# The rest of the modulation of a diffusion block: its weight chunks in buffers of their own

## The chip, the cores and the metric

One core of one Trainium2 chip. Times are device microseconds (us) of one execution, median of the runs shown. The engines are named as in the profile: PE (TensorE, with PEld for its weight loads), DVE (VectorE), ACT (ScalarE), POOL (GpSimd) and SP (SyncE, which here only issues DMA transfers).

## The reference

One layer of a diffusion model on 256 latent tokens with 256 context tokens, width 2048, in fp32. A conditioning vector gives six modulation rows; they enter at three places of the layer:

```python
silu_c = jax.nn.silu(c)
mod_l = jnp.split((silu_c @ w_mod[l] + b_mod[l])[:, None, :], 6, axis=-1)
...
y_ctx, y_lat = token_mixer(modulate(ctx, mod_c[0], mod_c[1]), modulate(x, mod_l[0], mod_l[1]),
                           rows, need_ctx, w_in[l], hy_p, ml_p, s5_p, out_p)
x = layer_norm(DEEPNORM_ALPHA * x + mod_l[2] * y_lat, ln1_g[l], ln1_b[l])
x = layer_norm(DEEPNORM_ALPHA * x + mod_l[5] * sq_relu_mlp(modulate(x, mod_l[3], mod_l[4]), w_ff1[l], w_ff2[l]),
               ln2_g[l], ln2_b[l])
```

`w_mod` is 2048 x 12288. The mixer projects its input with `w_in`, runs three branches (Hyena: long convolution; mLSTM; S5: a state-space scan), and merges them: `merged = g_hy * (y_hy @ w_hy_out) + g_ml * (y_ml @ w_ml_out) + g_s5 * (y_s5 @ w_s5_out)`, then `merged @ w_out`. The MLP is `square(relu(h @ w1)) @ w2` with 8192 hidden units. The first two modulation rows are needed at once; `mod_l[2]` after `w_out`, `mod_l[3]` and `mod_l[4]` after the first layer norm, `mod_l[5]` after the MLP's first `w_ff2` block.

## The kernel before, in words

All weights come from DRAM in chunks of 128 partitions x 1024 columns, 512 KB each, and are used once. A chunk of a matmul's weights is loaded by SP (`raw`, L200) into a tile `wr`, of which the pool `wp` has four buffers. ACT rounds it to the matmul's type (`wh`, L190), DVE subtracts to keep the rest (`wl`, L194), and PE does three products for each pair of operands, 24 matmuls of 256 columns for one chunk (L211). A `wr` buffer comes free when ACT and DVE have read it.

The rest of the modulation, rows 2 to 5 (8192 columns, 16 blocks of 512 columns, 8 chunks to a block, 128 chunks), does not go to PE as weights: it is a product with one vector. DVE does it, two instructions for a chunk, each 128 x 512: `acc = w * c` (L1178) for the first, `acc = w * c + acc` (L1180) for the others, called "macs" below. The sum over partitions is one matmul with ones into `px`, and the block's result goes to `mrow` in DRAM or to `mcol` (L1189, L1197). The chunk's load is the same `raw`, so it takes one of the four `wr` buffers. There is one accumulator tile, `mac`.

`mod_late` is a generator; `chunk_done` advances it after each weight chunk of the matmuls, by a rate that the stages set (0.3 to 1.75 chunks for each weight chunk). In what order the instructions then stand on each engine is decided by a scheduler, which simulates the program while it is built; each engine works in its order, SP's transfers too.

The stages that matter here, in order of time: pool pB holds the Hyena columns of `w_in`, the injection of inputs into the scan (`s5_inject`, last copy to the scan's inputs at L641), the scan itself (63 steps of four POOL instructions, L651 to L654; its first reader on DVE is L679, on PE L686), gate columns, and the scan's output with a gated linear unit. Pool pC holds the Hyena convolutions, the rest of the gate columns and three merges (products at L1231 and L1233). The tail, with pool ffp, does `w_out` (`residual`, L1276 and L1277, reads x in a `wr` tile, L1270), the first norm (aggregate L1288), ff1 and ff2 (`relu2`, with the square at L1354). The code asks for modulation blocks where they are used: `need_mods(12)` at the head of the tail, `drain(1)` between ff1 and ff2.

Of the kernel before, what the change touches and what calls it, by code (L numbers as in the profile page):

```python
# [17 lines left out]
P = 128  # L18
# [97 lines left out]
class Kern:  # L116
    def __init__(self, ctx, tc, I, out, dbg=None):
        self.tc, self.nc, self.I, self.out, self.dbg = tc, tc.nc, I, out, dbg or {}
        pool = lambda name, bufs, **k: ctx.enter_context(tc.tile_pool(name=name, bufs=bufs, **k))
        self.ctx = ctx  # L120
        self.cst = pool("cst", 1)
        self.wp = pool("wp", 3)
        self.t32p = pool("t32p", 2)
        self.sm = pool("sm", 2)
        self.ps = pool("ps", 2, space=bass.MemoryType.PSUM)
        self.dr = pool("dr", 1, space=bass.MemoryType.DRAM)
        self.n = 0
        self.sides = [[None, 0.0, 0.0] for _ in range(3)]
        self.bank, self.both = "aux", False
        self.mods = 0  # L130


    def nm(self, s):
# [1029 lines left out]
    def mod_late(self):  # L1163


        nc = self.nc
        v = nc.vector
        w = self.I["w_mod"][0]
        for b in range(16):
            c0 = 2 * D + b * 512  # L1170
            acc = self.t(self.sm, [P, 512], "mac", 1)
            for k0 in range(0, KT, 2):
                wt = self.raw(w, k0, 2, c0, 512)
                for kk in range(2):
                    k = k0 + kk
                    x, c = wt[:, kk], self.sc[:, k:k + 1]
                    if k == 0:
                        v.tensor_scalar(acc, x, c, None, op0=ALU.mult)  # L1178
                    else:
                        v.scalar_tensor_tensor(acc, x, c, acc, op0=ALU.mult, op1=ALU.add)  # L1180
                if k0 + 2 < KT:
                    yield
            which = b // 4
            if which in (0, 3):
                ps = self.aux([1, 512], "px")
                self.mm(ps, self.ones, acc, True, True)
                brow = self.b2([1, 512])
                nc.gpsimd.dma_start(brow, self.I["b_mod"][0:1, c0:c0 + 512])
                v.tensor_add(brow, brow, ps)  # L1189
                o = (b % 4) * 512  # L1190
                nc.gpsimd.dma_start(self.mrow[which // 3:which // 3 + 1, o:o + 512], brow)
            else:
                ps = self.aux([P, 4], "px")
                for j in range(4):
                    self.mm(ps[:, j:j + 1], acc[:, j * P:(j + 1) * P], self.ones, j == 0, True)
                o = (b - 4) * 4
                v.tensor_add(self.mcol[:, o:o + 4], ps, self.bmod[:, 32 + b * 4:36 + b * 4])  # L1197
            self.mods = b + 1
            yield

    def need_mods(self, n):
        while self.mods < n:
            next(self.sides[1][0])
# [42 lines left out]
    def tail(self, merged):  # L1246
        nc, I = self.nc, self.I
        v = nc.vector
        self.ffp = self.ctx.enter_context(self.tc.tile_pool(name="ffp", bufs=1))
        self.need_mods(12)  # L1250
        m2 = self.row(self.mrow[0:1, :], "rowa")
        x1 = self.t(self.ffp, [P, 2, D], "x1")
# [153 lines left out]
    def run(self):  # L1406
# [56 lines left out]
        with self.scope("yp") as self.yp:  # L1463
# [49 lines left out]
                self.mlstm_out()  # L1513
            steps = self.lin_w_steps(w_in, O_MG, 3 * D, KT, lat, self.mg_consume)
            with self.scope("pB") as self.br:
                self.n6 = 5
                hy = self.lin_w_steps(w_in, O_HY, 3 * W, KT, lat, self.hy_consume)
                self.run_steps(hy, 6)
                self.s5_inject()
                self.sides[1][1] = 0.3  # L1520
                self.with_side(self.s5_scan(), 2)
                self.run_steps(hy, 36)
                self.run_steps(steps, 32)
                self.with_side(self.s5_output(), 0.6)
                self.run_steps(steps, 48)
                self.drain()
                self.s5_glu()
            with self.scope("pC") as self.br:
                self.n6 = 7
                self.hyena()  # L1530
                self.run_steps(steps, 96)
                self.merge(1, I["w_ml_out"][0], self.y_ml, first=True)
                self.merge(2, I["w_s5_out"][0], self.y_s5)
                self.merge(0, I["w_hy_out"][0], self.y_hy, last=True)
        self.tail((self.mh, self.ml))

    def run_steps(self, steps, n):
# [35 lines left out]
```

## Time and profile before

| | us |
|---|---|
| median of 3 runs | 2005.19 (2005.02 to 2005.46) |
| profiled execution | 2014.18 |
| its span | 2012.4 |
| PE busy | 1870.4 (93%) |
| DVE busy | 1300.5 (65%) |
| ACT busy | 803.2 (40%) |
| POOL busy | 361.7 (18%) |

Busy shares are means over the span; the span has stages with different limits. A wait is the idle time of an engine ahead of an instruction, put down to what came last. 455.92 MB were moved, 227 GB/s over the span.

### The profile page before, as it was taken

The numbers are of one execution on the slowest core, as the hardware profiler recorded it, in microseconds if no ns is written. First come the engines' busy times: TensorE is split into PE (matmuls) and PEld (weight loads), VectorE is DVE, ScalarE is ACT, GpSimd is POOL, SyncE is SP. The second block draws the span as 40 slices with busy tenths as digits, with TensorE's granted clock in tenths as the row PEclk, the third lists the DMA queues.
The fourth block names the chain that finished last, engine by engine and source line by source line (L and its number), as shares of the span: only waits on it lengthen the run. The fifth ranks groups of instructions, "written<-read, shape, count | busy, mean of one in ns | idle before, by whom it ended". The sixth has DMA issues, their size and how long they took to land.

```text
span 2012.4 us, 34496 instructions
## 1 busy us (share of the span) xinstructions
PE 1870.4 (93%) x13945; PEld 1707.4 (85%) x13945; DVE 1300.5 (65%) x1810; ACT 803.2 (40%) x1063; POOL 361.7 (18%) x534
## 2 busy tenths in 40 slices
PE   5888999999997995999889998999999999999996
PEld 1666988989997995999779877999988899998985
DVE  8985777647866553556786866766755555555556
ACT  2433324226543333544234533444433344444332
POOL 1221101000019994000452400400000000000001
PEclk7898999999998997999999998999999999999998
DMA  9997667775797765677657866577765566666553
GB/s 346 339 344 262 192 202 220 227 208 174 232 349 230 239 222 210 226 254 259 244 180 253 276 225 227 158 240 224 254 224 187 187 183 186 181 186 231 190 188 105
DMA packets 253472, 455.92 MB, mean 227 GB/s; under 512 B 28597, under 2 KB 75349, under 8 KB 251776
## 3 DMA queue, kind: packets, MB, share of 16 engines
q1 hardware_dynamic: 221824, 382.43, 59.4%
q0 software_dynamic: 14112, 50.83, 7.0%
q10 hardware_dynamic: 17376, 20.45, 3.1%
q8 instruction: 109, 1.79, 0.4%
q14 instruction: 51, 0.42, 0.1%
HBM read 424.75 MB, written 32.05 MB: 227 GB/s over the span
## 4 chain that ended last, share of the span: by engine, by line
PE 67%; DMA 10%; DVE 9%; POOL 8%; issue 3%; ACT 2%; SPq 0%; ACTq 0%; POOLq 0%; DVEq 0%
PE mm L211 59%; PE aux L211 4%; DMA wr<-in_w_mod_dram 4%; DVE wl L194 3%; DMA wr<-in_w_in_dram 2%; POOL sc L651 2%; POOL sc L653 2%; POOL sc L652 2%; POOL t L654 2%; DMA wr<-in_w_out_dram 1%; ACT wh L190 1%; PE px L406 1%; PE px L211 1%; PE aux L214 1%; DVE mac L1180 1%
## 5 line engine op out<-in xcount | busy, mean ns | idle before, releaser
L211 PE MATMUL mm<-t,wh 128*128 128x256 f32 x5888 | 1101.7, 288 | 29.0 <-ACT wh L190 18.1
L211 PEld LDWEIGHTS mm<-t,wh 128*128 128x128 f32 x5888 | 932.2, 194 | 49.6 <-ACT wh L190 19.9
L194 DVE TENSOR_TENSOR wl<-wr,wh 128x1024 fp32r<-128x1024 f32 (+1 forms) x517 | 649.6, 1263 | 385.9 <-ACT wh L190 385.4
L190 ACT ACTIVATE wh<-wr 128x1024 fp32r<-128x1024 f32 (+1 forms) x517 | 545.9, 1058 | 811.0 <-PE mm L211 580.6
L211 PE MATMUL mm<-t,wl 128*128 128x256 f32 x2944 | 847.6, 288 | 13.9 <-DVE wl L194 13.8
L211 PEld LDWEIGHTS mm<-t,wl 128*128 128x128 f32 x2944 | 570.1, 194 | 25.9 <-DVE wl L194 18.3
L1180 DVE SCALAR_TENSOR_TENSOR mac<-wr,vecs,mac 128x512 f32<-128x512 f32 x240 | 185.3, 772 | 156.5 <-DMA wr<-in_w_mod_dram 153.8
L211 PE MATMUL mm<-wh,t 128*128 128x512 f32 (+1 forms) x960 | 249.1, 349 | 0.2
L211 PEld LDWEIGHTS mm<-wh,t 128*128 128x128 f32 x960 | 169.0, 190 | 24.2 <-ACT wh L190 1.6
L211 PE MATMUL mm<-wl,t 128*128 128x512 f32 (+1 forms) x480 | 168.0, 350 | 5.5 <-DVE wl L194 5.5
L211 PE MATMUL mm<-wh,ff 128*128 128x512 f32 (+1 forms) x576 | 155.3, 358 | 0.0
L211 PEld LDWEIGHTS mm<-wh,ff 128*128 128x128 f32 x576 | 101.7, 188 | 17.6
L211 PEld LDWEIGHTS mm<-wl,t 128*128 128x128 f32 x480 | 91.3, 190 | 20.5 <-DVE wl L194 9.2
L211 PE MATMUL mm<-wl,ff 128*128 128x512 f32 (+1 forms) x288 | 103.0, 357 | 0.0
L211 PE MATMUL mm<-ty,wh 128*128 128x256 f32 x384 | 73.3, 289 | 0.0
L1402 POOL DMA_DIRECT2D t<-in_ln_g_dram x1 | 0.5, 535 | 355.0 <-PE mm L211 355.0
L211 PE MATMUL mm<-ty,wl 128*128 128x256 f32 x192 | 56.4, 294 | 7.6 <-DVE wl L194 7.5
L211 PEld LDWEIGHTS mm<-wl,ff 128*128 128x128 f32 x288 | 54.2, 188 | 8.8
L211 PEld LDWEIGHTS mm<-ty,wh 128*128 128x128 f32 x384 | 60.7, 192 | 0.9
L406 PE MATMUL px<-wr,b 128*32 128x512 f32 x128 | 41.4, 739 | 18.1 <-DVE s5t L335 10.5
L211 PE MATMUL aux<-t,t 128*128 128x384 f32 (+3 forms) x160 | 47.3, 411 | 7.7 <-DVE t L1146 3.2
L211 PEld LDWEIGHTS mm<-ty,wl 128*128 128x128 f32 x192 | 36.9, 192 | 9.1 <-DVE wl L194 8.4
(384 smaller groups left out, 1621.6 us busy)
## 6 DMA issues: line engine op xcount, KB each, us to landing
wr<-in_w_ff_dram SPq DMA_DIRECT2D x256, 512.0 KB, 3.9
wr<-in_w_in_dram SPq DMA_DIRECT2D x192, 512.0 KB, 4.7
wr<-in_w_mod_dram SPq DMA_DIRECT2D x160, 512.0 KB, 4.8
wr<-in_w_out_dram SPq DMA_DIRECT2D x32, 512.0 KB, 4.7
wh<-in_w_mod_dram SPq DMA_DIRECT2D x16, 512.0 KB, 7.6
wl<-in_w_mod_dram SPq DMA_DIRECT2D x16, 512.0 KB, 7.1
QD<-s5Q POOLq DMA_DIRECT2D x12, 512.0 KB, 7.1
WA<-s5wa POOLq DMA_DIRECT2D x24, 256.0 KB, 6.2
```

The costliest lines, as they stand in the source:

```text
L190: return self.nc.scalar.activation(out, in_, f, bias=bias, scale=scale)
L194: self.nc.vector.tensor_sub(lo, x, hi.bitcast(F32))
L211: self.nc.tensor.matmul(out, lhsT, rhs, start=start, stop=stop, skip_group_check=True)
L214: self.nc.tensor.transpose(out, in_, self.c("ident", n)[:, :n])
L406: nc.tensor.matmul(ps[o:o + 32], self.st[:, k, :], raw[:, kk, :], start=k < 4, stop=k >= KT - 4, skip_group_check=True, tile_position=(0, o))
L651: v.tensor_mul(t1, self.a8[:, 0], S[:, :, :, :, n - 1])
L652: v.tensor_mul(t2, self.a8[:, 1], S[:, :, ::-1, :, n - 1])
L653: v.tensor_add(t1, t1, S[:, :, :, :, n])
L654: v.tensor_add(S[:, :, :, :, n], t1, t2)
L1180: v.scalar_tensor_tensor(acc, x, c, acc, op0=ALU.mult, op1=ALU.add)
L1402: nc.gpsimd.dma_start(g2r, I["ln2_g"].to_broadcast([P, D]))
```

## The change

Modulation chunks get a tile of their own, `wm`, from the pool of the stage: two buffers in pB, one in pC, two in the tail. Outside these stages (`modp` is None) they use `wr` as before. The four `wr` buffers then hold only the matmuls' weights (and x). In pB one line that set the number of `t6` buffers goes; no `t6` tile is taken there. 77 of the 128 modulation loads use `wm`: 38 in pB, 16 in pC, 23 in the tail. The lines of the new file from L131 on are one higher, from `mod_raw` on ten; the load of `wm` is L1208.

```diff
--- before.py
+++ after.py
@@ -128,6 +128,7 @@
         self.sides = [[None, 0.0, 0.0] for _ in range(3)]
         self.bank, self.both = "aux", False
         self.mods = 0
+        self.modp = None
 
 
     def nm(self, s):
@@ -1170,7 +1171,7 @@
             c0 = 2 * D + b * 512
             acc = self.t(self.sm, [P, 512], "mac", 1)
             for k0 in range(0, KT, 2):
-                wt = self.raw(w, k0, 2, c0, 512)
+                wt = self.mod_raw(w, k0, c0)
                 for kk in range(2):
                     k = k0 + kk
                     x, c = wt[:, kk], self.sc[:, k:k + 1]
@@ -1198,6 +1199,15 @@
             self.mods = b + 1
             yield
 
+    def mod_raw(self, w, k0, c0):
+
+        if self.modp is None:
+            return self.raw(w, k0, 2, c0, 512)
+        pool, bufs = self.modp
+        raw = self.t(pool, [P, 1024], "wm", bufs).rearrange("p (k c) -> p k c", k=2)
+        self.nc.sync.dma_start(raw, w[k0 * P:(k0 + 2) * P, c0:c0 + 512].rearrange("(k p) c -> p k c", p=P))
+        return raw
+
     def need_mods(self, n):
         while self.mods < n:
             next(self.sides[1][0])
@@ -1247,6 +1257,7 @@
         nc, I = self.nc, self.I
         v = nc.vector
         self.ffp = self.ctx.enter_context(self.tc.tile_pool(name="ffp", bufs=1))
+        self.modp = (self.ffp, 2)
         self.need_mods(12)
         m2 = self.row(self.mrow[0:1, :], "rowa")
         x1 = self.t(self.ffp, [P, 2, D], "x1")
@@ -1513,7 +1524,7 @@
                 self.mlstm_out()
             steps = self.lin_w_steps(w_in, O_MG, 3 * D, KT, lat, self.mg_consume)
             with self.scope("pB") as self.br:
-                self.n6 = 5
+                self.modp = (self.br, 2)
                 hy = self.lin_w_steps(w_in, O_HY, 3 * W, KT, lat, self.hy_consume)
                 self.run_steps(hy, 6)
                 self.s5_inject()
@@ -1525,13 +1536,16 @@
                 self.run_steps(steps, 48)
                 self.drain()
                 self.s5_glu()
+                self.modp = None
             with self.scope("pC") as self.br:
                 self.n6 = 7
+                self.modp = (self.br, 1)
                 self.hyena()
                 self.run_steps(steps, 96)
                 self.merge(1, I["w_ml_out"][0], self.y_ml, first=True)
                 self.merge(2, I["w_s5_out"][0], self.y_s5)
                 self.merge(0, I["w_hy_out"][0], self.y_hy, last=True)
+                self.modp = None
         self.tail((self.mh, self.ml))
 
     def run_steps(self, steps, n):
```

The scheduler makes other orders of it. Ahead of the scan's first reader (L679, after L680) on DVE, before the change (`mac` is the accumulator, the number a block or tile):

```order
L194 TENSOR_TENSOR wl_8242<-wr_8239,wh_8241 128x1024
L1197 TENSOR_TENSOR mcol_79<-px_8145,vecs_93 128x4
L1178 TENSOR_SCALAR mac_8352<-wr_8353,vecs_93 128x512
L194 TENSOR_TENSOR wl_8272<-wr_8269,wh_8271 128x1024
L1180 SCALAR_TENSOR_TENSOR mac_8352<-wr_8353,vecs_93,mac_8352 128x512
L194 TENSOR_TENSOR wl_8360<-wr_8357,wh_8359 128x1024
L1180 SCALAR_TENSOR_TENSOR mac_8352<-wr_8553,vecs_93,mac_8352 128x512
L194 TENSOR_TENSOR wl_8390<-wr_8387,wh_8389 128x1024
L1180 SCALAR_TENSOR_TENSOR mac_8352<-wr_8553,vecs_93,mac_8352 128x512
L194 TENSOR_TENSOR wl_8473<-wr_8470,wh_8472 128x1024
L679 TENSOR_TENSOR b_1109_8182<-t_677_5292,sign_85 64x4x32 x4
```

The same place after the change:

```order
L195 TENSOR_TENSOR wl_8360<-wr_8357,wh_8359 128x1024
L1181 SCALAR_TENSOR_TENSOR mac_8352<-wm_8790,vecs_93,mac_8352 128x512
L195 TENSOR_TENSOR wl_8390<-wr_8387,wh_8389 128x1024
L1181 SCALAR_TENSOR_TENSOR mac_8352<-wm_8790,vecs_93,mac_8352 128x512
L1181 SCALAR_TENSOR_TENSOR mac_8352<-wm_8885,vecs_93,mac_8352 128x512
L195 TENSOR_TENSOR wl_8473<-wr_8470,wh_8472 128x1024
L1181 SCALAR_TENSOR_TENSOR mac_8352<-wm_8885,vecs_93,mac_8352 128x512
L195 TENSOR_TENSOR wl_8560<-wr_8557,wh_8559 128x1024
L1181 SCALAR_TENSOR_TENSOR mac_8352<-wm_8986,vecs_93,mac_8352 128x512 x2
L195 TENSOR_TENSOR wl_8597<-wr_8594,wh_8596 128x1024
L1181 SCALAR_TENSOR_TENSOR mac_8352<-wm_9110,vecs_93,mac_8352 128x512 x2
L680 TENSOR_TENSOR b_1109_8182<-t_677_5292,sign_85 64x4x32 x4
```

Over the same number of rows, macs of two chunks stood among the subtractions ahead of the reader, and of four now; two more subtractions stand there than before (`wl_8560`, `wl_8597`).

At the head of the `w_out` stage, DVE before the change (`mac_11442` is the last block that `need_mods(12)` asks for, `mac_12364` the first of the last four, `t_1571` the merged operand):

```order
L194 TENSOR_TENSOR wl_12247<-wr_12244,wh_12246 128x1024
L194 TENSOR_TENSOR wl_12275<-wr_12272,wh_12274 128x1024
L194 TENSOR_TENSOR t_1571_11762<-t_1344_10182,t_1571_11762 128x1024
L1189 TENSOR_TENSOR b_1642_12268<-b_1642_12268,px_12266 1x512
L194 TENSOR_TENSOR wl_12293<-wr_12290,wh_12292 128x1024
L194 TENSOR_TENSOR wl_12311<-wr_12308,wh_12310 128x1024
L194 TENSOR_TENSOR wl_12331<-wr_12328,wh_12330 128x1024
L1178 TENSOR_SCALAR mac_12364<-wr_12365,vecs_93 128x512
L1180 SCALAR_TENSOR_TENSOR mac_12364<-wr_12365,vecs_93,mac_12364 128x512
L194 TENSOR_TENSOR wl_12349<-wr_12346,wh_12348 128x1024
L194 TENSOR_TENSOR wl_12383<-wr_12380,wh_12382 128x1024
L194 TENSOR_TENSOR wl_12401<-wr_12398,wh_12400 128x1024
```

After the change, from the same subtraction on:

```order
L195 TENSOR_TENSOR wl_12247<-wr_12244,wh_12246 128x1024
L195 TENSOR_TENSOR wl_12275<-wr_12272,wh_12274 128x1024
L1181 SCALAR_TENSOR_TENSOR mac_11442<-wm_12262,vecs_93,mac_11442 128x512
L195 TENSOR_TENSOR t_1571_11762<-t_1344_10182,t_1571_11762 128x1024
L1181 SCALAR_TENSOR_TENSOR mac_11442<-wm_12262,vecs_93,mac_11442 128x512
L195 TENSOR_TENSOR wl_12293<-wr_12290,wh_12292 128x1024
L195 TENSOR_TENSOR wl_12311<-wr_12308,wh_12310 128x1024
L1190 TENSOR_TENSOR b_1642_12268<-b_1642_12268,px_12266 1x512
L1179 TENSOR_SCALAR mac_12364<-wm_12365,vecs_93 128x512
L195 TENSOR_TENSOR wl_12331<-wr_12328,wh_12330 128x1024
L1181 SCALAR_TENSOR_TENSOR mac_12364<-wm_12365,vecs_93,mac_12364 128x512
L1181 SCALAR_TENSOR_TENSOR mac_12364<-wm_12470,vecs_93,mac_12364 128x512
```

The last two macs of `mac_11442`, which stood ahead of this place before, now stand behind two subtractions of `w_out`'s chunks, and the next block's first mac stands behind four subtractions of `w_out` instead of five.

SP's queue at the same place, before:

```order
L1270 DMA wr_12326<-in_x_dram 128x2x512
L200 DMA wr_12328<-in_w_out_dram 128x2x512
L200 DMA wr_12346<-in_w_out_dram 128x2x512
L200 DMA wr_12365<-in_w_mod_dram 128x2x512
L200 DMA wr_12380<-in_w_out_dram 128x2x512
L200 DMA wr_12398<-in_w_out_dram 128x2x512
L200 DMA wr_12416<-in_w_out_dram 128x2x512
L200 DMA wr_12434<-in_w_out_dram 128x2x512
L200 DMA wr_12452<-in_w_out_dram 128x2x512
L200 DMA wr_12470<-in_w_mod_dram 128x2x512
L200 DMA wr_12474<-in_w_out_dram 128x2x512
L1270 DMA wr_12492<-in_x_dram 128x2x512
```

After:

```order
L1208 DMA wm_12262<-in_w_mod_dram 128x2x512
L1208 DMA wm_12365<-in_w_mod_dram 128x2x512
L1281 DMA wr_12326<-in_x_dram 128x2x512
L201 DMA wr_12328<-in_w_out_dram 128x2x512
L1208 DMA wm_12470<-in_w_mod_dram 128x2x512
L201 DMA wr_12346<-in_w_out_dram 128x2x512
L201 DMA wr_12380<-in_w_out_dram 128x2x512
L201 DMA wr_12398<-in_w_out_dram 128x2x512
L1208 DMA wm_12577<-in_w_mod_dram 128x2x512
L201 DMA wr_12416<-in_w_out_dram 128x2x512
L1208 DMA wm_12673<-in_w_mod_dram 128x2x512
L201 DMA wr_12434<-in_w_out_dram 128x2x512
```

Where two modulation loads stood among twelve transfers, five do now; the first two follow each other. Counted over the whole order on DVE: between the last merge product and the norm's first aggregate there are 8 macs before and 43 after; between the aggregate and ff1's first square 2 before and 7 after; behind that square 38 before and none after. Between the last state-input copy (L641) and the first reader of the scan there are 28 before and 41 after; while the inputs are injected 6 and 13. On PE, 46 weight chunks stand between the injection's last matmul and the scan's first reader before, 49 after. The number of instructions on each engine stays the same.

## Rows read from the trace of the kernel before

**Rows 1.** page, part 4: shares of the chain that ended last

```profile
PE 67%; DMA 10%; DVE 9%; POOL 8%; issue 3%; ACT 2%; SPq 0%; ACTq 0%; POOLq 0%; DVEq 0%
```

**Rows 2.** busy time by stage; columns PE, PEld, DVE, ACT, POOL, PEclk, DMA share, GB/s

```profile
545.00:600.00 55.00, 53.82 (x724) 52.57 (x724) 35.89 (x86) 28.29 (x57) 5.40 (x8) 1.00 1.00 344
600.00:780.00 180.00, 143.65 (x1148) 141.06 (x1148) 95.35 (x97) 59.85 (x74) 164.95 (x270) 0.91 0.64 211
...
930.00:1150.00 220.00, 196.96 (x1469) 184.99 (x1468) 167.75 (x200) 89.14 (x116) 83.38 (x85) 0.97 0.72 239
1150.00:1248.00 98.00, 88.63 (x462) 73.94 (x460) 63.28 (x79) 35.97 (x35) 3.89 (x4) 0.97 0.69 223
1248.00:1290.00 42.00, 35.20 (x254) 32.97 (x255) 37.98 (x57) 22.52 (x40) 26.07 (x20) 0.87 0.51 162
```

**Rows 3.** PE's waits, 600 to 780 us: total, times, longest

```profile
PE aux L686 <- POOL sc L651: 21.4, 1, 21.4
```

**Rows 4.** POOL's instructions, 601 to 778 us: busy us, mean ns | idle before

```profile
L652 POOL TENSOR_TENSOR sc<-t 128x96 f32<-128x96 f32 x63 | 44.0, 698 | 0.0
L653 POOL TENSOR_TENSOR sc<-sc,t 128x96 f32<-128x96 f32 x63 | 42.7, 678 | 0.1
L651 POOL TENSOR_TENSOR sc<-t 128x96 f32<-128x96 f32 x63 | 42.0, 666 | 7.8 <-DVE t L641 3.2
L654 POOL TENSOR_TENSOR t<-sc,sc 128x96 f32<-128x96 f32 x63 | 31.0, 493 | 4.5
```

**Rows 5.** timeline, 632 to 635.3 us: start, duration

```profile
631.75 0.40 PE L211 MATMUL mm<-t,wh 128*128 128x256 f32 x2
...
632.11 0.40 PE L211 MATMUL mm<-t,wh 128*128 128x256 f32 x2
...
632.12 2.79 DVE L194 TENSOR_TENSOR wl<-wr,wh 128x1024 fp32r<-128x1024 f32 x2
...
633.79 1.43 POOL L652 TENSOR_TENSOR sc<-t 128x96 f32<-128x96 f32 x1
```

**Rows 6.** timeline of POOL, 770 to 774 us, no DVE work beside it

```profile
773.05 0.44 POOL L652 TENSOR_TENSOR sc<-t 128x96 f32<-128x96 f32 x1
```

**Rows 7.** DVE's waits, 930 to 1150 us

```profile
DVE mac L1180 <- DMA wr<-in_w_mod_dram: 29.9, 11, 5.0
```

**Rows 8.** PE's waits, 930 to 1150 us

```profile
PE mm L211 <- DVE wl L194: 15.3, 9, 4.1
```

**Rows 9.** DVE's instructions, 1150 to 1248 us: busy us, mean ns | idle before

```profile
L194 DVE TENSOR_TENSOR wl<-wr,wh 128x1024 fp32r<-128x1024 f32 x33 | 42.0, 1276 | 24.6 <-ACT wh L190 24.5
...
L1180 DVE SCALAR_TENSOR_TENSOR mac<-wr,vecs,mac 128x512 f32<-128x512 f32 x7 | 5.3, 751 | 7.2 <-DMA wr<-in_w_mod_dram 7.1
```

**Rows 10.** DMA issues, 1150 to 1248 us: count, KB each, median us to landing

```profile
wr<-in_w_mod_dram SPq DMA_DIRECT2D x4, 512.0 KB, 5.2
```

**Rows 11.** DMA issues, 550 to 600 us

```profile
wr<-in_w_mod_dram SPq DMA_DIRECT2D x4, 512.0 KB, 7.5
```

**Rows 12.** timeline of DVE: four squares of the MLP, L1354

```profile
1289.69 1.22 DVE L1354 TENSOR_TENSOR b<-b 128x1024 f32<-128x1024 f32 x1
...
1453.96 1.21 DVE L1354 TENSOR_TENSOR b<-b 128x1024 f32<-128x1024 f32 x1
...
1655.70 1.22 DVE L1354 TENSOR_TENSOR b<-b 128x1024 f32<-128x1024 f32 x1
...
1816.98 1.22 DVE L1354 TENSOR_TENSOR b<-b 128x1024 f32<-128x1024 f32 x1
```

**Rows 13.** timeline of DVE at both ends of the w_out stage

```profile
1146.73 1.22 DVE L194 TENSOR_TENSOR wl<-wr,wh 128x1024 fp32r<-128x1024 f32 x1
1147.87 0.74 DVE L1180 SCALAR_TENSOR_TENSOR mac<-wr,vecs,mac 128x512 f32<-128x512 f32 x1
1148.53 1.28 DVE L1233 TENSOR_TENSOR mg<-mm,mg 128x512 f32<-128x512 f32 x2
...
1248.20 0.58 DVE L1288 BATCH_NORM_AGGREGATE l1mv<-lnst 128x2 f32<-128x48 f32 x2
```

## The prediction

> **What bounds the kernel now.** I read the chain of waits first: TensorE (PE) makes 67% of the chain that ended last, DMA 10%, VectorE (DVE) 9% and GpSimd (POOL) 8% [rows 1]. So the kernel is a matmul stream whose gaps are made by late weight chunks, by DVE, and once by the state-space scan on POOL. Then I read the busy time by stage, since the average over the span hides where each limit stands [rows 2]. The reader is to see three kinds of stage there. In 545 to 600 us the DMA share is 1.00 at 344 GB/s: nothing more can be fetched. In 600 to 780 POOL is busy 164.95 of 180 us with the scan, and PE waits 21.4 us at one place for its last step [rows 3]. In 930 to 1150 (hyena, gate columns, merges) and 1150 to 1248 (`w_out`) PE has 23 us and 9.4 us of gaps, and no engine is full. In ff1 (1289.69 to 1453.96) 7 blocks take 164.3 us, against 161.3 us for the same 7 blocks from 1655.70 to 1816.98 [rows 12], so the modulation work that lies in ff1 costs at most 3 us there.
>
> The two ops a chunk of the rest of the modulation ("macs", 0.75 us each) wait for their load: in 930 to 1150 DVE stands 29.9 us in 11 waits for one [rows 7], in 1150 to 1248 another 7.1 us [rows 9].
>
> **What the change does.** No instruction is added or taken away. 77 of the 128 modulation loads (38 in pB, 16 in pC, 23 in the tail) leave the rotation of four `wr` buffers for one of their own, two buffers deep (one in pC). The scheduler then places loads and macs earlier. Counted from the orders: 38 macs stand behind the first relu2 of ff1 before and none now; between the last merge product and the norm's first aggregate there are 8 before and 43 now. So the question is what the macs cost in the stages into which they move.
>
> *Scan.* Between the last state-input copy and the scan's first reader on DVE stand 28 macs before and 41 now, and 2 more `wl` subtractions. Beside DVE's subtraction of 1.40 us a scan step takes 1.43 us [rows 5], alone 0.44 [rows 6]: 0.99 us lost, 0.71 of DVE's time. The whole scan says the same: 159.7 us for 252 steps [rows 4], where 252 of 0.44 are 110.9 us, so 49 us are lost to DVE. 13 macs × 0.75 and 2 × 1.40 us are 12.5 us of DVE work, times 0.71 is 8.9 us by which the scan ends later. But PE's order has 3 more weight chunks ahead of the scan's first reader (49 for 46). Matmuls start three to 0.36 us [rows 5], so 24 of a chunk take 2.88 us, three 8.6 us: PE has that much more to do inside the 21.4 us for which it now waits. I take **0**; from below −6 (the scan is not slowed by macs that fall into gaps of its own) to +4 (macs block it for their whole length).
>
> The row shows a step that loses 0.71 of the DVE instruction beside it. The Trainium skill, page "SBUF — State Buffer", section "Who interferes with whom", says that a DVE instruction with two SBUF inputs contends with a GpSimd instruction that reads SBUF, and that the loser of that lock blocks for the other's whole instruction. By it the added DVE work would cost 12.5 us in place of 8.9, and this term would be +3.9 in place of 0; the trace lies under the rule.
>
> *Injection into the scan's state.* 7 more macs (13 for 6), so 3.5 more loads of 512 KB (1.8 MB) are asked of a stretch at 344 GB/s [rows 2], in which a load lands 7.5 us after its issue [rows 11]: 1.8 MB are 5.3 us of a full DMA. The loads are only earlier, the weight chunks' turn comes later, and part is made up in 600 to 780, where the share is 0.64. I take **+1** (0 to +5).
>
> *Hyena and merges.* The macs there are about as many as before. With one buffer a load cannot start before the second mac of the chunk ahead is done, so the wait for landing stays; the 29.9 us of DVE waits [rows 7] should not shrink much. What improves is the weight side: four `wr` buffers hold weights alone. PE loses 15.3 us to late `wl` [rows 8]. I take about half of that, **−7**; the bounds are −20 (both kinds of waits shrink) and +5 (a load that waits for its single buffer holds the weight loads behind it on SP).
>
> *`w_out`.* This is the largest term. DVE is busy 63.28 of 98 us [rows 2], with 24.5 us of waits for `wh` and 7.1 for loads [rows 9]: 95 of 98. 35 more macs at 0.72 us (between the 0.75 of one and the 0.67 from start to start) are 25 us, so DVE is busy 88 of 98 before any wait. Now the waits. Two buffers mean that a load is issued at the earliest when the second mac two chunks earlier is done, and it lands 5.2 us later [rows 10]. In the new order of DVE, in ten of the twenty such gaps of the stage, two subtractions and two macs stand between; started back to back these take 2 × 1.14 + 2 × 0.67 = 3.6 us (starts of ops that touch: 1146.73 to 1147.87 and 1147.87 to 1148.53 [rows 13]), so DVE stands about 1.6 us each time, 15 us in all; the first load of the stage is issued behind four loads of `w_out` and adds about 5. So 88 + 20 = 108 us for 98: **+10**. The bounds: 0, if the subtractions' old waits and these are the same gaps seen from the other side, as far as PE's 88.63 us of busy time permits; +22, if landing rises from 5.2 to 7.5 us, because 18 more loads are 9.4 MB in 98 us, which takes 223 GB/s to about 319, near the 344 at which the DMA was full [rows 2].
>
> *Norm.* PE is short of work here, 35.20 of 42 us [rows 2], and waits for DVE and ACT. Between the aggregate and ff1's first square stand 7 macs for 2; 5 of 0.75 us are **+4** (+1 to +8, beside POOL's 26 us of multiplies, where an op on DVE may be stretched as the subtraction of 1.40 us was).
>
> *ff1.* The 38 macs are gone: **−3** [rows 12]. Nothing more is to be had, as PE never stops.
>
> Sum: 0 + 1 − 7 + 10 + 4 − 3 = **+5 us**. The profiled execution took 2014.18 us with a span of 2012.4, and the median of the runs is 2005.19, so 9 us lie between profile and timing. The terms are a few waits each and do not grow with that, so I put the sum on the median: **2010 us** (and about 2019 in a profiled execution).
>
> **The rivals.** *Faster:* loads in buffers of their own run ahead of their macs. What speaks for it: the waits of 29.9 and 7.1 us are just those that a deeper prefetch removes, and in `w_out` DVE has 35 us of gaps to hold 25 us of macs. The chain holds waits for modulation loads only as a part of DMA's 10%. Price: half of PE's gaps in 930 to 1248 go (32/2 = 16) with −3 in ff1 and the scan's reader unchanged, +4 left in the norm: −15, 1990 us; all gaps gone, about −30. It decides where the DVE waits in `w_out` stay under the 10 us that DVE has left (98 − 88). Against it: two buffers are 3.6 us of lead for 5.2 us of landing.
> *Same:* gains in pC and ff1 meet the loss in `w_out`, or PE, 88.63 of 98 us, hides half of it: −7 + 1 + 5 + 4 − 3, within 4 us of 2005.
> *Slower by more:* DMA fills in `w_out`. At a landing of 7.5 us the ten short gaps are 2.3 us longer each, 23 us; half of it may fall together with weight chunks that are as late, so this term is +22 in place of +10. With +4 more in the injection: about 2026 us.
> *The scan blocked for whole instructions:* the scan ends 12.5 us later, while PE has 8.6 us more to do; +4 on the sum, 2014 us. The 1.43 us step beside a subtraction of 1.40 speaks against it. This is the rule of the Trainium skill's page "SBUF — State Buffer" cited above.
> *The change does nothing:* the loads would have to be held back by something other than buffers. The orders differ at 77 loads, so no more than a few hundredths.
>
> **How the numbers follow.** 0.2% (4 us) is about what a measurement can tell from no change. My forecast (+5, from +4 to +14) gets 0.32, the DMA-full case 0.12, the blocked scan 0.05: slower 0.49. Same 0.17, with the change that does nothing inside. Faster 0.34, since the waits that the change aims at are real, and a model in which DVE's old and new waits add up may count one gap twice. The range reaches from 1987, past the faster case's middle of 1990, to 2031, past the DMA-full case; the likeliest case's own is 2009 to 2019.
>
> **What would show it.** Right: 1150 to 1248 grows to about 108 us between the last merge product (1148.53) and the first aggregate (1248.20) [rows 13], with DVE over 80% busy, waits of mac for `wm` of 15 to 25 us, and DMA near 320 GB/s; seven blocks of ff1 at 161 us; the wait for the scan's last step smaller by about as much as the weight chunks took; PE's wait for `wl` in the hyena and merges under 10 us. Wrong: `w_out` at 98 us or less with few waits for `wm` (then two buffers were enough, and the faster case holds), a landing of 7 us there (then the DMA is full), or a scan that ends over 10 us later with PE idle. What would make the whole prediction wrong is above all that the macs fit into DVE's gaps in `w_out`, as then the largest term is gone and the sum falls to −5.

## The result, and the profile after

The changed kernel takes 2023.34 us (median of 5 runs, 2022.75 to 2026.8) where the kernel before takes 2005.02 (2003.93 to 2005.46): ratio 1.0096, 95% interval 1.0082 to 1.0111. It is 18 us slower. The direction was forecast and the time lies in the stated range (1987 to 2031), but the forecast was 2010: the sum of +5 us is less than a third of what came, and 2023 lies outside the 2009 to 2019 that the likeliest case was given.

The first profiled execution of the kernel before (2014.18 us) lay 9 us above its median, so I profiled it once more (e1 below: 2008.01 us, span 2006.2). From here on "before" in a comparison of stages is that second profile, where the first is not named. The span after is 2021.6, 15.4 us more, and the stages, cut at the same instructions in both, give it to the tail:

| stage, from instruction to instruction | before (e1) | after | difference |
|---|---|---|---|
| start to last copy of the scan's inputs | 599.2 | 601.0 | +1.8 |
| to the last product of the gated linear unit | 341.7 | 342.1 | +0.4 |
| to the last merge product | 204.4 | 202.0 | −2.4 |
| `w_out`: to the first aggregate | 96.1 | 106.8 | +10.7 |
| norm: to ff1's first square | 41.2 | 51.7 | +10.5 |
| ff1: to its 8th square | 165.7 | 159.9 | −5.8 |
| the rest | 557.9 | 558.1 | +0.2 |

The chain that ended last, page of the changed kernel (against [rows 1]: DMA's share falls from 10 to 6%, PE's rises):

```profile
PE 71%; DVE 9%; POOL 9%; DMA 6%; issue 3%; ACT 2%; POOLq 0%; DVEq 0%; ACTq 0%; SPq 0%
```

Busy time by stage of the changed kernel, to be set beside [rows 2]; columns as there:

```profile
545.00:600.00 55.00, 55.00 (x736) 53.80 (x735) 37.18 (x87) 25.30 (x50) 3.43 (x5) 1.00 1.04 370
600.00:785.00 185.00, 147.72 (x1180) 144.41 (x1181) 111.44 (x117) 63.11 (x79) 174.01 (x274) 0.92 0.70 230
...
930.00:1146.00 216.00, 194.47 (x1445) 183.64 (x1444) 169.82 (x196) 87.11 (x114) 86.66 (x85) 0.96 0.72 238
1146.00:1252.00 106.00, 93.30 (x476) 76.39 (x474) 85.82 (x115) 36.36 (x35) 2.34 (x4) 0.96 0.91 301
1252.00:1304.00 52.00, 39.33 (x268) 37.40 (x269) 44.27 (x63) 22.71 (x40) 27.90 (x22) 0.82 0.44 146
1304.00:1464.00 160.00, 160.00 (x1317) 158.51 (x1316) 85.08 (x72) 71.30 (x69) 1.03 (x2) 1.00 0.64 192
```

The reader is to see `w_out` (fourth line here): DVE busy 85.82 of 106 us where it was 63.28 of 98, and DMA at 301 GB/s where it was 223. The norm (fifth) holds 10 us more, PE is idle for a larger part of it, and the mean granted clock of the stretch is 0.82 where it was 0.87.

The same stages of e1, the second profile of the kernel before:

```profile
1145.30:1241.40 96.10, 88.58 (x466) 73.24 (x464) 63.62 (x81) 36.46 (x35) 4.59 (x4) 1.00 0.70 232
1241.40:1282.60 41.20, 34.58 (x252) 32.28 (x253) 38.55 (x57) 22.34 (x40) 26.33 (x20) 0.88 0.49 160
1282.60:1448.30 165.70, 164.22 (x1335) 160.43 (x1335) 109.82 (x112) 72.05 (x70) 1.01 (x2) 1.00 0.74 238
```

The waits of DVE in `w_out` after the change, and what it did there (against [rows 9]):

```profile
DVE mac L1181 <- DMA wm<-in_w_mod_dram: 12.4, 9, 3.3
DVE wl L195 <- ACT wh L191: 7.1, 9, 1.7
```

```profile
L195 DVE TENSOR_TENSOR wl<-wr,wh 128x1024 fp32r<-128x1024 f32 x33 | 41.2, 1255 | 7.1 <-ACT wh L191 7.1
L1181 DVE SCALAR_TENSOR_TENSOR mac<-wm,vecs,mac 128x512 f32<-128x512 f32 x40 | 29.9, 748 | 12.8 <-DMA wm<-in_w_mod_dram 12.4
```

24.5 us of waits for `wh` have become 7.1, 5.3 us of macs 29.9. A `wm` load lands in 5.0 us, as a modulation load did before [rows 10]:

```profile
wm<-in_w_mod_dram SPq DMA_DIRECT2D x21, 512.0 KB, 5.0
```

At the end of `w_out` one of these waits stands in the way. PE's last product, DVE's next instructions:

```profile
1243.71 0.28 PE L212 MATMUL mm<-wh,t 128*128 128x256 f32 x1
```

```profile
1246.77 0.75 DVE L1181 SCALAR_TENSOR_TENSOR mac<-wm,vecs,mac 128x512 f32<-128x512 f32 x1 [3.29 <-DMA wm<-in_w_mod_dram]
1247.43 0.75 DVE L1287 TENSOR_TENSOR b<-mm,rowa 128x256 f32<-128x256 f32 x2
```

The product is done at 1243.99, but DVE reads it (`residual`, L1287) only at 1247.43, behind a mac that waited 3.29 us for its load.

In the norm the macs stand between the pieces that PE's transposes and products wait for, while POOL multiplies. DVE's timeline there, then POOL's:

```profile
1257.58 0.74 DVE L1181 SCALAR_TENSOR_TENSOR mac<-wm,vecs,mac 128x512 f32<-128x512 f32 x1
...
1260.19 1.78 DVE L1181 SCALAR_TENSOR_TENSOR mac<-wm,vecs,mac 128x512 f32<-128x512 f32 x1
1261.89 1.85 DVE L195 TENSOR_TENSOR t<-b,t 128x256 fp32r<-128x256 f32 x2
1263.66 1.77 DVE L1181 SCALAR_TENSOR_TENSOR mac<-wm,vecs,mac 128x512 f32<-128x512 f32 x1
```

```profile
1258.71 2.71 POOL L1351 TENSOR_TENSOR x<-x,rowa 128x512 f32<-128x512 f32 x2 [3.02 <-PE aux L215]
1262.01 2.87 POOL L1352 TENSOR_TENSOR x<-x,rowb 128x512 f32<-128x512 f32 x2 [0.59 <-DMA rowb<-in_ln_b_dram]
```

A mac that starts before POOL's multiplies takes 0.74 us; those that start 0.24 or 0.25 us after one of them take 1.77 or 1.78. PE then waits for DVE's pieces, 9.2 us in all after its first transposes against 3.5 in e1, and behind such waits its granted clock falls. Two of the waits, and the clock (the third column from the right) after the first of them:

```profile
1275.71 0.58 PE L212 MATMUL mm<-t,wh 128*128 128x256 f32 x1 [2.12 <-DVE t L195]
1287.58 0.39 PE L212 MATMUL mm<-t,wh 128*128 128x256 f32 x1 [2.53 <-DVE t L195]
```

```profile
1275.70:1280.70 5.00, 4.99 (x23) 4.99 (x24) 2.22 (x4) 0.72 (x2) 0.00 (x0) 0.50 0.71 204
```

The clock is at 0.50, the level of 1.2 GHz, from 1274.4 to 1281.2 and again from 1288.1 to 1291.5 us. In e1 it stays at 1.00, 2.4 GHz, from 1251.4 us to the end of the norm:

```profile
1251.40:1282.60 31.20, 28.06 (x227) 26.97 (x226) 29.60 (x28) 16.43 (x28) 22.81 (x17) 1.00 0.38 110
```

### The profile page after: what moved, and what is told of

It reads as the page before. It is cut to its first block, busy times and chain, and to the rows that moved or that the text cites. A ratio compares the mean times of both kernels' runs of the same rounds, so it can differ in the third digit from the quotient of the medians.

```text
span 2021.6 us, 34510 instructions
## 1 busy us (share of the span) xinstructions
PE 1872.2 (93%) x13945; PEld 1710.2 (85%) x13945; DVE 1309.8 (65%) x1810; ACT 801.2 (40%) x1063; POOL 371.4 (18%) x534
## 4 chain that ended last, share of the span: by engine, by line
PE 71%; DVE 9%; POOL 9%; DMA 6%; issue 3%; ACT 2%; POOLq 0%; DVEq 0%; ACTq 0%; SPq 0%
PE mm L212 62%; PE aux L212 4%; DMA wm<-in_w_mod_dram 3%; DVE wl L195 2%; POOL t L655 2%; POOL sc L654 2%; POOL sc L652 2%; POOL sc L653 2%; DVE mac L1181 1%; DMA wr<-in_w_out_dram 1%; PE px L407 1%; PE px L212 1%; ACT wh L191 1%; PE aux L215 1%; DMA t<-kd 1%
## 5 line engine op out<-in xcount | busy, mean ns | idle before, releaser
L1181 DVE SCALAR_TENSOR_TENSOR mac<-wm,vecs,mac 128x512 f32<-128x512 f32 x149 | 124.8, 837 | 38.6 <-DMA wm<-in_w_mod_dram 37.0
L1181 DVE SCALAR_TENSOR_TENSOR mac<-wr,vecs,mac 128x512 f32<-128x512 f32 x91 | 68.0, 748 | 21.1 <-DMA wr<-in_w_mod_dram 19.7
L212 PE MATMUL aux<-t,t 128*128 128x384 f32 (+3 forms) x160 | 48.6, 423 | 10.2 <-ACT b L191 3.0
```

Of the source, the lines that this page charges most:

```text
L212: self.nc.tensor.matmul(out, lhsT, rhs, start=start, stop=stop, skip_group_check=True)
```

## The experiments

The first question was which of the three buffers costs the time, and whether the first profile of the kernel before can be trusted for stages.

**e1**, the kernel before, unchanged. 

> The kernel before, once more with a profile. Its first profiled execution took 2014 us against a median of 2005, so the two traces differ by 9 us while the medians differ by 18. Theory one (the 9 us are a chance loss of the first profile): this profile comes out at 2004 to 2007, and the stage that is 9 us shorter than in the first profile shows where the change costs more than the two first traces say. Theory two (profiling costs this kernel 9 us each time): it comes out at 2013 to 2015 with the same stages.

Measured: one execution, 2008.01 us, span 2006.2, against a median of 2005.65 in 23 runs beside it, whose extremes are 1997.88 and 2012.51. Theory one, in the main, though 1 us above its band: the first profile was a long execution (span 2012.4). Theory one looked for the difference in one stage; it is spread: 2.5 us ahead of the scan, 1.3 more up to the last merge product, 3.0 in `w_out`. The stage lengths of the norm (41.5 and 41.2) and of ff1 (164.3 and 165.7) agree.

**e2**, own buffers in pB and pC, the tail on `wr`:

```diff
-        self.modp = (self.ffp, 2)
```

> Own buffers in pB and pC only; the tail's modulation loads go back to wr. Theory one (the loss is in the tail, where macs now stand in w_out and beside GpSimd's multiplies in the norm): 2001 to 2006, the same as before or a little faster. Theory two (a good part of it is the scan, which macs slow down): 2010 or more.

Measured: 2006.59 us, ratio 0.9999 (0.9986 to 1.0013). Theory one. The scan lasts from 599.7 to 782.2 us there, longer than in e1 (599.3 to 774.7), and the gated unit ends at 941.7 us against 940.9.

**e3**, own buffers in the tail only (the lines of pB and pC taken out). 

> Own buffers in the tail only. Theory one: w_out about 8 us longer, norm about 10 us longer, ff1 about 4 us shorter, so 2017 to 2022. Theory two: the tail alone gives at most half of the loss, 2005 to 2014.

Measured: 2021.68 us, ratio 1.0069 (1.0052 to 1.0085). Theory one: in its trace `w_out` lasts 108.7 us, the norm 51.6 and ff1 159.4, as in the changed kernel. By ratio the tail costs 14 us of the 19; by span nearly all of it (2020.8 against 2021.6).

**e4**, own buffers in pB only. 

> Own buffers in pB only. Theory one: 2003 to 2007, the scan ends some 7 us later and the weight chunks done meanwhile give it back by the end of pB. Theory two: 2010 or more, the later end of the scan is not given back.

Measured: 2006.91 us, ratio 1.0005 (0.9994 to 1.0017). Theory one again: the scan's first reader comes 181.7 us after the last copy of the scan's inputs (174.0 in e1), the gated unit's end 342.8 us after it (341.7).

So the tail is the cause. The next two runs divide it into its stages and into work and loads.

**e5**, nothing of the modulation in the norm:

```diff
-                wt = self.mod_raw(w, k0, c0)
+                wt = self.mod_raw(w, k0, c0, self.late if b == 15 and k0 >= 8 else None)
...
+        if after is not None:
+            self.nc.vector.tensor_copy(raw[:, 0, 0:1], after)
```

`late` is a value that the first square of ff1 leaves. 

> The changed kernel, but the last four modulation chunks wait for ff1's first square: no mac stands in the norm (7 in the changed kernel), 42 stay in w_out, 8 go to ff1. Theory one (macs in the norm are stretched by GpSimd's multiplies and sit in the chain ahead of PE's transposes): the norm is 9 to 10 us shorter, 41 to 43 us as before, ff1 about 1 us longer, and the kernel takes 2012 to 2016. Theory two (the longer norm is a fetch of ff1's weights that comes late, since the DMA was busy with modulation chunks): the norm stays at 48 us or more and the kernel above 2018.

Measured: 2012.02 us, ratio 1.0033 (1.0022 to 1.0045). Theory one. The stages, `w_out`, norm and ff1 in this order:

```profile
1144.40:1252.40 108.00, 95.61 (x484) 77.49 (x482) 86.81 (x116) 37.14 (x36) 4.07 (x5) 0.97 0.88 292
1252.40:1293.70 41.30, 33.88 (x252) 31.46 (x253) 39.13 (x57) 22.06 (x40) 28.07 (x22) 0.90 0.49 152
1293.70:1454.60 160.90, 160.90 (x1328) 159.60 (x1328) 90.82 (x86) 72.17 (x70) 0.49 (x1) 1.00 0.66 198
```

The norm is back at 41.3 us, `w_out` is still 108.0, and ff1 takes the 8 macs for 1.0 us at most, with PE busy all along (160.90 of 160.90). Seven macs in the norm cost two thirds of the whole loss by ratio (1.0096 to 1.0033).

**e6**, the tail's loads all there, its macs narrow:

```diff
-                        v.scalar_tensor_tensor(acc, x, c, acc, op0=ALU.mult, op1=ALU.add)
+                        v.scalar_tensor_tensor(acc[:, :n], x[:, :n], c, acc[:, :n], op0=ALU.mult, op1=ALU.add)
```

> The changed kernel with all loads of the tail in their own buffers, in the same order, but each mac of the last blocks save the first of a block works on 1 column instead of 512 (the rest of the modulation row is left out). Theory one (DVE's time for the macs makes w_out longer: busy 88 of 98 us and waits on top): w_out comes back to 96 to 100 us and the norm to 42, so the kernel takes 1998 to 2004. Theory two (the 21 further loads in w_out fill the DMA and hold the weight chunks back): w_out stays at 104 us or more, the kernel above 2010.

Measured: 2008.43 us, ratio 1.0005 (0.9991 to 1.0019). Above the band that theory one gave for the total, but by stage it is theory one: `w_out` 98.0 us, the norm 43.9.

```profile
1144.60:1242.60 98.00, 91.22 (x483) 76.42 (x481) 66.82 (x116) 37.42 (x36) 3.85 (x5) 0.99 0.94 327
1242.60:1286.50 43.90, 34.69 (x252) 32.87 (x253) 38.77 (x63) 22.35 (x40) 27.07 (x22) 0.87 0.53 180
```

```profile
DVE wl L195 <- ACT wh L191: 17.8, 17, 2.2
DVE mac L1182 <- DMA wm<-in_w_mod_dram: 11.3, 8, 3.3
```

The DMA moves more (327 GB/s), `wm` loads land later (6.1 us by the profile's issue rows), DVE waits about as long for them (11.3 us), and the stage is 9 us shorter than with wide macs. Where these 9 us lie is seen by cutting the stage at PE's last product. From the last merge product to there it is 92.2 us in e1, 98.9 in the changed kernel (102.6 or 102.7 in e3, e5 and e8, whose `w_out` has the same macs) and 92.4 here: neither the traffic nor the waits lengthen this part, DVE's busy time does, 86 against 67 us over the stage. From PE's last product to the aggregate it is 3.9 us in e1, 7.9 in the changed kernel (5.3 to 6.2 in e3, e5 and e8) and 5.6 here. In this part a mac's wait for its load counts in full when it stands ahead of `residual`, 3.29 us in the changed kernel's profile and 1.0 to 1.4 in the other three. The narrow macs still take 8.9 us in all, so the loads and they together are priced here at about 2 us (98.0 against 96.1).

**e7**, no mac beside the scan (tail on `wr`):

```diff
-                self.sides[1][1] = 0.3
+                self.sides[1][1] = 0.0
                 self.with_side(self.s5_scan(), 2)
...
+                self.late = self.S[:, 0, 0, 0, NCH - 1:NCH]
+                self.sides[1][1] = 0.7
```

> Tail on wr, pB and pC own, and no mac between the injection and the scan's first reader: these loads wait for the scan's last step, and 68 macs stand between the scan and the gated unit (18 in the changed kernel). Theory one (a mac costs the scan 0.7 of its length, and PE waits for the scan's end): the scan lasts 150 to 160 us instead of 183, PE's wait for it falls from 26 us to under 8, and the kernel takes 1988 to 2000. Theory two (DVE's subtractions alone set the scan's length, or the 50 further macs after it come back as waits): scan above 168 us, or 2003 to 2010 all the same.

Measured: 2002.24 us, ratio 0.9969 (0.9952 to 0.9986), faster than both kernels, but neither theory's case: from its first to its last instruction's start the scan takes 166.5 us (175.4 in e1) instead of 150 to 160, and PE's wait for it is 21.2 us, as long as in e1 (21.4) and not under 8.

```profile
PE aux L688 <- POOL sc L653: 21.2, 1, 21.2
```

PE reaches the place where it waits earlier too, at 745 us against 753 in e1. Behind the scan DVE then waits for modulation loads:

```profile
DVE mac L1182 <- DMA wm<-in_w_mod_dram: 38.6, 19, 8.7
```

and the stretch from the scan's first reader to the end of the gated unit is 177.4 us long (765.2 to 942.6) against 167.8 in e1. What the scan gains is given back there.

**e8 and e9**, the changed kernel and the kernel before without POOL's 16 multiplies and adds in the norm. 

> The changed kernel without GpSimd's 16 multiplies and adds of the first norm's gain and offset (they are left out). Theory one (DVE is stretched beside them): the macs in the norm take 0.75 us instead of up to 1.78, and the norm is 4 to 8 us shorter than 51.7. Theory two (the macs cost their place in the order only): the norm is shorter by less than 3 us.

 

> The kernel before without GpSimd's 16 multiplies and adds of the first norm's gain and offset (they are left out), for the changed kernel without them, whose norm lasted 38.7 us. Theory one (most of the longer norm is macs stretched by GpSimd): the norm lasts 33 to 36 us, so that without GpSimd's work the 7 macs cost 3 to 5 us instead of 10. Theory two (the cost is the place of the macs in the order alone): 28 to 30 us, the same 10 us of difference.

Measured, the norm of each, changed kernel first:

```profile
1250.90:1289.60 38.70, 34.25 (x258) 33.34 (x259) 28.88 (x63) 21.86 (x40) 3.17 (x6) 0.85 0.60 200
```

```profile
1241.40:1277.20 35.80, 32.30 (x252) 31.09 (x253) 24.80 (x56) 22.31 (x40) 2.20 (x4) 0.90 0.61 206
```

In the changed kernel every mac of the norm takes 0.69 to 0.75 us then, and the granted clock does not fall again once it is up, at 1262.6 us. Without POOL's work the macs cost 2.9 us of stage (38.7 − 35.8); with it 10.5 (51.7 − 41.2). Theory one in both, and e8's own gain, 13 us, is more than it gave. These are single executions, but the difference of the differences, 7.6 us, is well above what the norm varies by: it lasts 41.1 to 44.4 us in the seven profiles of kernels whose tail uses `wr` and keeps POOL's work. The 7.6 us are not all stretched macs, which lose 3.6 us by themselves (8.8 us for seven, 5.2 without POOL's work, by the two traces); the rest is what follows from them, PE's waits and its slower clock, and no run divides it.

**e10**, e7 with four buffers in pB. 

> As the kernel with no mac beside the scan, with four buffers instead of two in pB. There DVE waited 45 us for modulation loads between 760 and 945 us. Theory one (these waits hold up the weight chunks behind them): they halve, and the kernel is 3 to 8 us faster than with two buffers, 1992 to 1998. Theory two (PE is full there anyway): no change, 1998 to 2003.

Measured: 2000.39 us, ratio 0.9969 (0.9957 to 0.9981). By the timing theory two: no change against e7, by ratio. DVE's waits for `wm` by L1182 fell from 38.6 to 7.6 us in that stretch; it waits 34.9 us for `wh` instead. In both versions a gain of 0.3% against the kernel before is shown; the traces do not say with one voice where it lies. Against e1, e7 is 8 us ahead at the scan's first reader and behind by 1.7 at the gated unit's end; e10 starts its scan 6 us earlier, and keeps that.

**e11**, e10 with fewer chunks behind the scan:

```diff
-                self.sides[1][1] = 0.7
+                self.sides[1][1] = 0.45
```

> As the kernel with no mac beside the scan and four buffers, with a lower rate of modulation chunks after the scan (46 macs between scan and gated unit instead of 70, 52 in ff1 instead of 36). Theory one (macs crowd the stage after the scan): 3 to 6 us faster than at the higher rate with four buffers. Theory two: the macs in ff1 cost as much as they save, the same within 3 us.

Measured: 2026.71 us, ratio 1.01 (1.0087 to 1.0114). Neither theory. Up to the 8th square it runs as e10 (1442.5 against 1441.0 us); then the 16 macs of the last block follow one another where ff1 ends, with little between them, because the code finishes the modulation there at once, and the loads that ff2 needs first stand behind theirs in SP's queue. PE's waits, 1440 to 1700 us, and the stretch 1440 to 1500:

```profile
PE mm L213 <- ACT wh L192: 17.0, 1, 17.0
```

```profile
1440.00:1500.00 60.00, 42.50 (x171) 32.48 (x170) 35.55 (x39) 18.94 (x18) 1.52 (x3) 0.83 0.66 218
```

SP waits 16.0 us for macs in 1436 to 1462: the loads of ff2's first chunks stand behind modulation chunks that fill the `wr` buffers.

## Why the prediction was right or wrong

**The bound and the direction** held: a stream of matmuls, lengthened where DVE becomes late. By mechanism the likeliest case was the one that came, but its size was wrong. That 2023 lies near the 2026 of the DMA-full rival is chance: that rival's mechanism did not come.

***w_out*, +10.** Measured +10.7 against the second profile (+7.7 against the first). Busy time 86 of 107 us where 88 was forecast, waits for `wm` 12.4 where I had 20, DMA 301 GB/s where I had 319. By e6 the busy time is what counts up to PE's last product: nearly the same waits with narrow macs cost nothing there. Only the wait behind it, 3.3 us ahead of `residual`, counts as it stands. So I had the right sum by a wrong split, and that is luck: 20 us of waits for `wm` were no term of their own, and those for `wh`, which I had let go to nothing, kept 7.1 of 24.5 us.

***Norm*, +4: the step that failed.** Measured +10.5. I counted 5 more macs of 0.75 us and named the stretching beside POOL only as an upper bound, +8. The trace has 6 macs from 1256 us on at a mean of 1.35 us (8.1 us), and PE waiting for the scaled pieces behind them. e5 takes the macs away and has 41.3 us; e9 and e8 show that 7.6 of the 10.5 us are there only while POOL multiplies. The sum also had no term for the clock: with two falls it is at 0.50 for 10.2 us in which PE, where it has work, does half of what it does at 1.00 (three products start in 0.64 us instead of 0.36); by that it costs up to 5 us, an estimate from these rows. The row from which I could have had it stood in my own scan term, a step of 1.43 us instead of 0.44 beside a subtraction: I used it for POOL and did not turn it round for DVE. By the Trainium skill, page "SBUF — State Buffer", section "Who interferes with whom", the port pair that DVE and GpSimd share is an exclusive lock, and the order of issue decides which of the two blocks. The trace agrees: the macs of 1.77 and 1.78 us, 1.03 more than alone, start 0.24 or 0.25 us after a multiply of 1.47 us and end 0.5 us after its end, so here DVE is the one that waits.

***Hyena and merges*, −7.** Measured −2.4. PE's waits for `wl` fell from 15.3 [rows 8] to 11.3 us, not by half; DVE's for modulation loads from 29.9 [rows 7] (27.4 in e1) to 16.9, which I had held fixed:

```profile
PE mm L212 <- DVE wl L195: 11.3, 7, 3.2
```

```profile
DVE mac L1181 <- DMA wm<-in_w_mod_dram: 16.9, 9, 4.7
```

PE's other waits in the stretch rose meanwhile, from 6.9 us in e1 to 10.2, so most of what `wl` gave up came back as waits for other pieces of DVE and ACT. I read the effect of four free `wr` buffers too high. Between the profiles the sum missed 10.4 us (15.4 for 5): this term has 4.6 of them, the norm's 6.5, and the other errors nearly cancel.

***Scan*, 0.** Measured +0.4 up to the end of the gated unit. POOL's scan steps took 167.4 us against 159.7 [rows 4], +7.7 where 8.9 was forecast:

```profile
L654 POOL TENSOR_TENSOR sc<-sc,t 128x96 f32<-128x96 f32 x63 | 44.2, 701 | 0.0
L655 POOL TENSOR_TENSOR t<-sc,sc 128x96 f32<-128x96 f32 x63 | 42.2, 671 | 4.6
L653 POOL TENSOR_TENSOR sc<-t 128x96 f32<-128x96 f32 x63 | 41.5, 659 | 0.0
L652 POOL TENSOR_TENSOR sc<-t 128x96 f32<-128x96 f32 x63 | 39.5, 626 | 7.2 <-DVE t L642 3.0
```

The sign that I gave to know it by was wrong: PE's wait for the scan's last step did not shrink, it grew from 21.4 us to

```profile
PE aux L687 <- POOL sc L652: 25.8, 1, 25.8
```

The chunks that PE does ahead of this place are not to be done behind it, and by the end of the gated unit, where also fewer macs stand (18 for 28), the later end of the scan is made up. The rival of whole-instruction blocking (+4) did not come by the end of that stretch.

***Injection*, +1.** +1.8 up to its end; the stage itself is longer by 5.8 us (550.5 to 601.0 against 554.5 to 599.2) and starts 4.0 earlier, probably because macs moved into it from ahead of it. The DMA moved 370 GB/s from 545 to 600 us, so the 344 GB/s at a share of 1.00 [rows 2] was not the most that can be fetched, as I had read it.

***ff1*, −3.** Measured −5.8 (−4.4 against the first profile): 7 blocks in 159.9 us, less than the 161.3 of the later blocks [rows 12] that I took for the floor. The floor holds: PE is full, and at ff1's first square, which comes late behind the macs, it has done 13 more of ff1's products than in e1 (233 for 220 since the aggregate), 1.6 us at 0.12 each. So about 1.6 us of the norm's +10.5 and of ff1's −5.8 are one shift of the border between them.

**The rivals.** Faster did not come: the macs did not fit into DVE's gaps in `w_out`, nor in the norm. DMA-full did not come either: a landing of 5.0 us, and e6 at 327 GB/s is hardly slowed.

**What stays open:** the medians differ by 18 us, the spans of the profiles by 15; and the tail alone gives 14 us by ratio while its span is nearly that of the changed kernel. Executions of the kernel before, run beside the experiments, spread over 1997.88 to 2013.68 us, more than this gap, and no run here settles it. How the norm's loss divides into stretched macs, their place in the order and PE's clock is open too.

## What to carry to other kernels

A buffer of its own lets a scheduler move work forward into stages where it did not stand: count where it lands, stage by stage, before counting the waits it loses. Five more instructions of 0.75 us placed into a stretch where another engine makes them wait and where PE waits on each piece cost 10 us; the same work in a stage where PE was full cost at most 1 us for 8 of them. Sum the busy time of the engine that feeds PE; its waits for loads need not come on top, except where one stands directly ahead of what the next stage needs. And look at what PE's granted clock does behind new waits.

## What the runs showed of the hardware

In the norm DVE waits for POOL's instruction to end; it does not just run more slowly beside it. In e6 a mac of the norm works on one column. Ahead of POOL's work it takes 0.16 to 0.22 us, beside it 1.18 to 1.20, up to the end of POOL's multiply; first a free one, then one beside a multiply, then that multiply:

```profile
1243.24 0.22 DVE L1182 SCALAR_TENSOR_TENSOR mac<-wm,vecs,mac 128x1 f32<-128x1 f32 x1
...
1256.15 1.18 DVE L1182 SCALAR_TENSOR_TENSOR mac<-wm,vecs,mac 128x1 f32<-128x1 f32 x1
```

```profile
1256.06 1.26 POOL L1352 TENSOR_TENSOR x<-x,rowa 128x512 f32<-128x512 f32 x1
```

The mac started 0.09 us after the multiply and ended 0.01 us after it (1257.33 and 1257.32). That is probably part of why the norm of e6 does not come back to e1's length with macs this narrow (43.9 against 41.2): three of its macs take 1.2 us each.

With no mac beside the scan (e7) there are stretches in which the scan falls into step with DVE's subtractions: one scan step for each weight chunk, its last add beside the subtraction and 1.47 us long, the other three at their lone 0.44 or 0.45. The timeline of POOL and DVE in one:

```profile
666.40 0.45 POOL L655 TENSOR_TENSOR sc<-sc,t 128x96 f32<-128x96 f32 x1
666.91 1.23 DVE L196 TENSOR_TENSOR wl<-wr,wh 128x1024 fp32r<-128x1024 f32 x1 [1.66 <-ACT wh L192]
666.93 1.47 POOL L656 TENSOR_TENSOR t<-sc,sc 128x96 f32<-128x96 f32 x1
668.48 0.44 POOL L653 TENSOR_TENSOR sc<-t 128x96 f32<-128x96 f32 x1
...
669.79 1.23 DVE L196 TENSOR_TENSOR wl<-wr,wh 128x1024 fp32r<-128x1024 f32 x1 [1.65 <-ACT wh L192]
669.80 1.47 POOL L656 TENSOR_TENSOR t<-sc,sc 128x96 f32<-128x96 f32 x1
```

From one add to the next 2.87 us pass, the 2.88 of a chunk. Of the scan's 63 steps 34 have a last add of over 1.2 us. Over the whole scan these adds take 963 ns in the mean in e7, where they took 493 [rows 4], and the other three kinds 451 to 501 where they took 666 to 698. So the POOL instruction that starts 0.01 to 0.02 us after DVE's loses most of DVE's 1.23 us, and while it stays in this step the scan goes no faster than the chunks. That may be why taking 28 macs away shortened it by 9 us and not by 15 (28 × 0.75 × 0.71); no run here separates it.
